# Differential attention on one core: the order of the work in each attention unit is replaced by two fixed orders

## The chip, the cores and the metric

The kernel runs on one core of a Trainium2 chip. The metric is the device time of one execution in microseconds (us), lower is better. The core has a matrix engine (TensorE, PE in the profile), three engines for elementwise work (VectorE = DVE, ScalarE = ACT, GpSimd = POOL), and a queue for transfers (SyncE = SP). Each engine runs its own instructions in program order and waits on semaphores for the others. [...]

## The reference, cut to what matters

The program is a two-layer trunk (attention, MLP, S5, MLP). The change touches only layer 0's attention, which is differential attention: each head has two score maps, and the second softmax, times a factor, is subtracted from the first.

```python
s = jnp.einsum('bqhcd,bkhcd->bhcqk', q, k).astype(jnp.float32)   # c = 0, 1
p = jax.nn.softmax(s, axis=-1)
w = p[:, :, 0] - lam * p[:, :, 1]
o = jnp.einsum('bhqk,bkhe->bqhe', w.astype(v.dtype), v)
return rmsnorm(o, subln_g) * (1.0 - lambda_init)
```

There are 8 heads, 1024 latent tokens and 256 context tokens (1280 keys), and 128 value columns per head. Context queries see the context keys alone. The queries and keys of a head are projections of the normed input by 128 columns of `attn_w_qkv`, and those of latent tokens are rotated (rope).

## The kernel before

Every fp32 product is done as three fp32r matmuls of split operands (high and low half; `mm3`, lines 131 to 134), so each operand is split by `split` (line 137: a copy on ACT gives the high half; line 138: a subtraction on DVE or POOL gives the low half).

`phase_b` runs the attention. It goes through 72 units, `n = 9h + u`: per head `h` one unit `u = 0` for the 256 context queries and eight units `u = 1..8` of 128 latent queries each. Two units (1 and 2, 3 and 4, and so on) form a pair of 256 queries; `pair = (u+1)//2`. In a unit these things happen, and in this program's "manual" section the order in which they are written is the order on PE, DVE, ACT and POOL; transfers are issued on SP:

- **scores** (line 579): both score maps. Map 0 fills PSUM columns 0 to 1279 (banks 0, 1 and half of 2), map 1 columns 1792 to 3071 (half of bank 3, banks 4 and 5). 18 matmuls for u > 0, 12 small ones for u = 0.
- **maxima** (line 592, or 588 for u = 0): DVE copies each map to SBUF and takes its row minimum (queries are negated).
- **exps** (line 602, or 599): ACT takes the exponential of each map with its row sum.
- **combine** (lines 610, 611, 613): DVE forms `w = p0 - lam * p1` for all 1280 keys.
- **parts**: the weights `w` of the unit *before* are transposed by PE (`w_part`, lines 620 and 625) in three pieces: key tiles 0-3 (w0), 4-5 (w1), 6-9 (w2). w0 is split straight from PSUM by `w_direct` (631 ACT, 632 DVE); w1 and w2 are copied to SBUF by ACT (`w_copy`, 638) and split by POOL (641, 642).
- **values** (lines 132 to 134, 256 columns): for a finished pair, weights times V into columns 0 to 255 of bank 6 (`pb`); `pair_out` copies the result out (732, ACT), POOL squares it (733), and `pair_sums` sums the squares by two one-column matmuls into bank 6 (739) and a copy (740, ACT). Pairs 1, 2, 3 are due in units 4, 6, 8, pair 0 in unit 2, and pair 4 in unit 1 of the next head.
- **projections**: in units 0, 1, 2, 3, 5, 7 the next head's keys and queries are projected (`proj_group`, `AHEAD`), eight products of three matmuls into bank 7, in up to three slices called fills (`FILLS`). Groups of context tokens (units 1 and 2) are split `direct`ly (523 ACT, 524 DVE). The others go through `evac` (528 ACT and 529 DVE empty the bank, and four transfers swap halves), `sine` (534 POOL), `add` (537 DVE) and `store` (137 ACT, 138 DVE). These later steps are queued in `post` and taken by `next_post`.
- **norm_pair** (772 DVE, 137 ACT, 138 POOL, two transfers): the norm of the previous head's pairs, in units 7 and 8 and 0 to 2 of the next head, from head 1's unit 7 on.

Units 4, 6 and 8 have values and no projection (`inside`): w0 goes to bank 7 there, between the two halves of the values. In the other units w0 goes to columns 1280 to 1791 (`whole`: halves of banks 2 and 3), which the scores leave free but whose banks they share. In head 7 there is nothing left to project; from `n = 64` on the output projection of heads 0 to 5 (`wo_group`, bank 7, emptied by 851) takes the place of the projections.

Of the kernel before, what the change touches and what calls it, by code (L numbers as in the profile page):

```python
# [6 lines left out]
F32 = mybir.dt.float32  # L7
# [63 lines left out]
class Prog:  # L71
# [431 lines left out]
    def proj_group(self, h, T, g, wt):  # L503

        nc = self.nc
        n, c0 = self.G_TOK[g], (256, 768, 0)[g]
        b = self.qb.next()[:, 0:n]
        scale = 1.0 if T else -0.125
        t = slice(c0 - 256, c0 + 256)
        hT = self.hT[g]  # L510
        q, sw, qc = self.rq, self.rs, self.rc
        hi, lo = (self.stg[:, j, 0:n] for j in range(2)) if h == 0 else self.operand(h, T, g)

        def product(k):
            return lambda: self.mm3(b, wt[k][0], wt[k][1], hT[0][:, k], hT[1][:, k], k == 0, k == 7)

        def out():
            if h == 0:
                for j, x in enumerate((hi, lo)):
                    self.dma((self.Kd if T else self.Qd)[j, :, c0 : c0 + n], x.bitcast(F32))  # L520

        def direct():
            nc.scalar.activation(hi, b, AF.Copy, scale=scale)
            nc.vector.scalar_tensor_tensor(lo, b, scale, hi.bitcast(F32), ALU.mult, ALU.subtract)  # L524
            out()

        def evac():
            nc.scalar.activation(q, b, AF.Copy, scale=scale)
            nc.vector.scalar_tensor_tensor(qc, b, scale, self.cosT[:, t], ALU.mult, ALU.mult)
            for j in range(4):  # L530
                self.dma(sw[32 * j : 32 * j + 32], q[32 * (j ^ 1) : 32 * (j ^ 1) + 32])

        def sine():
            nc.gpsimd.tensor_tensor(sw, sw, self.sinT[:, t], ALU.mult)

        def add():
            nc.vector.tensor_tensor(qc, qc, sw, ALU.add)

        def store():
            self.split(hi, lo, qc)  # L540
            out()

        return [product(k) for k in range(8)], [direct] if g == 2 else [evac, sine, None, add, store]


    def lam_setup(self):
# [103 lines left out]

    WO_BANKS = {8: 0, 9: 1, 0: 2, 1: 3, 2: 4, 3: 5, 4: 7}
    AHEAD = {0: (1, 0), 1: (1, 2), 2: (0, 2), 3: (1, 1), 5: (0, 0), 7: (0, 1)}
    FILLS = {0: (0, 3, 8, 8), 1: (0, 0, 8, 8), 2: (0, 4, 8, 8)}

    def b_start(self):

        self.rq, self.rs, self.rc = self.fv(0, 512), self.fv(2, 512), self.fv(4, 512)
        self.cosT, self.sinT = self.wv(8, 1024), self.wv(12, 1024)
        self.raw = Ring([self.wv(0, 1024), self.wv(4, 1024)])
        self.wr = Ring([(self.rv(4 * i, 4, 128), self.rv(4 * i + 2, 4, 128)) for i in range(3)])  # L660
        self.stg = self.rv(12, 2, 512)
        self.qb = Ring([self.bank(i) for i in (4, 5)])
        splits = [self.proj_weights(0, 1), self.proj_weights(0, 0)]
        self.dma(self.cosT, self.I["cos_t"])
        self.dma(self.sinT, self.I["sin_t"])
        post = []
        for split, T in zip(splits, (1, 0)):
            split(0)
            wt = split(1)
            for g in (2, 0, 1):  # L670
                products, rest = self.proj_group(0, T, g, wt)
                for f in products:
                    f()
                for f in post:
                    f()
                rest[0]()
                post = [f for f in rest[1:] if f]
                yield
        for f in post:
            f()  # L680

    def phase_b(self):
# [38 lines left out]
        def values(h, pair, k0=0, k1=10):  # L721
            V = loaded[h, "v"]
            last = 2 if pair == 0 else 10
            for kt in range(k0, min(k1, last)):
                self.mm3(pb[:, 0:256], V[0][:, kt], V[1][:, kt], self.wT[0][:, kt], self.wT[1][:, kt],
                         kt == 0, kt == last - 1)
# [9 lines left out]

        def pair_sums(h, pair):
            for i in range(2):
                mm(pb[:, 256 + i : 257 + i], sq[:, 128 * i : 128 * i + 128], self.ones, start=True, stop=True)
            nc.scalar.activation(hst[:, 1, h, 2 * pair : 2 * pair + 2], pb[:, 256:258], AF.Copy)  # L740


        def norm_calc(h, q0=0, q1=10):
# [25 lines left out]
        def norm_pair(h, pair):  # L769
            i = nloaded.pop(0)  # L770
            (nob, nrb), (nhi, nlo) = nbufs[i], nsplit[i]
            nc.vector.scalar_tensor_tensor(nob, nob, self.sg, nrb, ALU.mult, ALU.mult)
            self.split(nhi, nlo, nob, nc.gpsimd)
            for j, t in enumerate((nhi, nlo)):
                self.dma(self.on[h, j, :, 256 * pair : 256 * pair + 256], t.bitcast(F32))

        cols7 = ((2, 0), (0, 0), (0, 256), (1, 0), (1, 256))
        buf6 = [(nob, nrb), (self.wv(6, 256), self.wv(7, 256))]
# [88 lines left out]
        def next_post():  # L867
            f = post.pop(0) if post else None
            if f:
                f()  # L870

        with self.manual():
            for n in range(72 + 5):
# [10 lines left out]
                if front:  # L884
# [6 lines left out]
                        groups = [self.proj_group(h + 1, *a, wts[a[0]]) for a in (self.AHEAD[u],)] if u in self.AHEAD else []  # L891
                    self.scores(u, queries(pair), Ks[h % 2])
                    self.maxima(u, p, sm)
                if front:
                    if u == 8 and h < 6 or n == 0:
                        qsplit = self.proj_weights(h + 2 if n else 1, 0)
                    if u == 5 and h < 6:
                        ksplit = self.proj_weights(h + 2, 1)
                if 64 <= n < 74:
                    groups = [wo_group(wo_order[n - 64])]  # L900
                fills = [[], [], []]
                if h >= 7 and groups:
                    a = (0, 2, 4, 6) if late else (0, 4, 6, 6)
                    fills = [groups[0][0][a[i] : a[i + 1]] for i in range(3)]
                elif groups:
                    a = self.FILLS.get(u, (0, 4, 8, 8))
                    fills = [groups[0][0][a[i] : a[i + 1]] for i in range(3)]

                def fill(i):
                    for f in fills[i]:  # L910
                        f()

                def part(i):
                    if i < parts:
                        tb = pb[:, 256:512] if i == 1 else self.bank(7) if i == 0 and not groups else self.PS[:, 1280:1792]
                        return self.w_part(prev[1], prev[2], i, tb)

                def copied(w):
                    return self.w_copy(*w) if w else lambda: None

                inside = late and not groups and parts == 3
                if pv:
                    values(*pv, 0, 5 if inside else 10)
                fill(0)
                if front:
                    self.exps(u, 0, p, sm, s0, sn)
                while sums and sums[0][0] <= n:
                    sums.pop(0)[1]()
                w0 = part(0)
                next_post()  # L930
                if parts == 3:
                    self.w_direct(*w0)
                if inside:
                    values(*pv, 5)
                w1 = part(1)
                w2 = part(2) if inside else None
                if front:
                    self.exps(u, 1, p, sm, s0, sn)
                if inside:
                    halves2 = copied(w2)  # L940
                if pv:
                    pair_out(*pv)
                    sums.append((n + 1, lambda a=pv: pair_sums(*a)))
                    if pv[0] == 7:
                        tail.append((n + 1, pv[1]))
                if inside:
                    halves2()
                if front:
                    self.combine(u, p, s0, sn)
                if parts == 1:  # L950
                    self.w_direct(*w0)
                copied(w1)()
                fill(1)
                if not inside:
                    copied(part(2))()
                fill(2)
                if front and n - 7 >= 9 and (n - 7) % 9 < 5 and (n - 7) // 9 < 7:
                    norm_pair((n - 7) // 9 - 1, (n - 7) % 9)
                rest = groups[0][1] if groups else [None]
                if len(rest) == 1 and rest[0]:  # L960
                    rest[0]()
                todo7, run7 = run7, []
                for f in todo7:
                    f.pop(0)()
                    if f:
                        run7.append(f)
                if front and u == 0:
                    next_post()
                next_post()
                if len(rest) > 1:  # L970
                    rest[0]()
                    post += rest[1:]
                if h < 7 and u < 2:
                    wts[0] = qsplit(u)
                if h < 6 and u in (6, 7):
# [491 lines left out]
    def halves(self, src, slot):  # L1467
        self.split(slot[:, 0], slot[:, 1], src)
        return slot
# [1129 lines left out]
```

## Time and profile before

| what | value |
|---|---|
| time, median of 3 runs | 2877.79 us (2875.0 to 2881.31) |
| the profiled execution's own time | 2875.86 us |
| its span in the profile | 2874.1 us |
| PE busy | 2726.4 us (95%) |
| DVE, ACT, POOL busy | 2027.9 (71%), 1367.3 (48%), 1051.3 (37%) |
| the attention units (first score matmul to the end of unit 71) | from 216.7 to about 882 us |

Rows of the profile give the line of the kernel, the engine, the operation, and output and inputs by tile names (PS is PSUM, F, FC, W and R are SBUF areas), then partitions x elements. "x" is a count. A busy PE is not PE at its peak, since matmuls are pipelined and their ends are modelled. A row "A <- B" of the waits says that A sat idle until B was done.

### The profile page before, as it was taken

Reading aid. Unit: us, or ns where it says so; the run is one execution under the profiler, and the core shown is the slowest. Engines: PE = TensorE matmul, PEld = TensorE weight load, DVE = VectorE, ACT = ScalarE, POOL = GpSimd, SP = SyncE. Lnnn points to the kernel's source line nnn. Section 1 sums busy time; section 2 is a strip of 40 time slices with the busy share of each in tenths; the row PEclk is TensorE's granted clock in tenths of the full one; section 3 lists DMA queues with packets and bytes.
Section 4 is the critical chain, followed back from the end, with each engine's and each line's share of the span. In section 5 each row is a group of like instructions: output and inputs, shape, how many; then the busy total and the mean of one; then the engine's idle time right before and its main releaser. Section 6 shows DMA issues by size and latency. Waiting matters only on the chain. (4 is left out here: it accounts for less than half of the span.)

```text
span 2874.1 us, 43751 instructions
## 1 busy us (share of the span) xinstructions
PE 2726.4 (95%) x15645; PEld 2258.7 (79%) x15645; DVE 2027.9 (71%) x2984; ACT 1367.3 (48%) x2584; POOL 1051.3 (37%) x902
## 2 busy tenths in 40 slices
PE   6999988899888999999999999899999999999999
PEld 4787877777777787878877778788887778878887
DVE  6357777777775477766698878799633597668566
ACT  3425555555553763333344445477443633344443
POOL 3315665666654710000030004588221243336414
PEclk9999999999999999999999999899999999999999
DMA  9953123222524448887699878479843144467544
GB/s 281 323 176 115 60 87 90 91 80 64 179 85 138 150 147 303 296 300 255 211 326 318 277 238 274 154 230 274 285 140 109 60 157 162 161 228 240 163 133 143
DMA packets 377448, 539.13 MB, mean 188 GB/s; under 512 B 38286, under 2 KB 231052, under 8 KB 374028
## 3 DMA queue, kind: packets, MB, share of 16 engines
q1 hardware_dynamic: 377228, 536.32, 57.5%
q8 instruction: 123, 2.02, 0.3%
q14 instruction: 97, 0.79, 0.1%
HBM read 367.54 MB, written 164.47 MB: 185 GB/s over the span
## 5 line engine op out<-in xcount | busy, mean ns | idle before, releaser
L132 PE MATMUL PS<-H 128*128 128x512 f32 x1072 | 420.7, 393 | 3.1 <-ACT H L137 2.3
L134 PE MATMUL PS<-H 128*128 128x512 f32 x1072 | 417.7, 390 | 3.4 <-DVE H L138 2.1
L133 PE MATMUL PS<-H 128*128 128x512 f32 x1072 | 417.9, 390 | 0.0
L132 PE MATMUL PS<-H,R 128*128 128x512 f32 (+1 forms) x828 | 307.9, 374 | 15.6 <-DVE R L524 11.7
L133 PE MATMUL PS<-H,R 128*128 128x512 f32 (+1 forms) x828 | 300.8, 363 | 0.0
L134 PE MATMUL PS<-H,R 128*128 128x512 f32 (+1 forms) x828 | 299.8, 363 | 0.0
L602 ACT ACTIVATE F<-F,stat 128x1280 f32<-128x1280 f32 x128 | 174.2, 1361 | 168.3 <-DVE F L592 168.2
L132 PEld LDWEIGHTS PS<-H 128*128 128x128 f32 x1072 | 201.2, 188 | 50.7 <-issue 6.2
L134 PEld LDWEIGHTS PS<-H 128*128 128x128 f32 x1072 | 201.2, 188 | 46.7 <-DVE H L138 2.9
L133 PEld LDWEIGHTS PS<-H 128*128 128x128 f32 x1072 | 201.3, 188 | 40.6
L132 PE MATMUL PS<-R,H 128*128 128x512 f32 x534 | 212.2, 398 | 6.0 <-ACT H L137 3.3
L137 ACT ACTIVATE H<-U 128x640 fp32r<-128x640 f32 x216 | 132.1, 675 | 174.0 <-PE PS L133 146.6
L137 ACT ACTIVATE R<-W 128x512 fp32r<-128x512 f32 (+1 forms) x185 | 129.6, 708 | 174.7 <-PE PS L133 107.9
L134 PE MATMUL PS<-R,H 128*128 128x512 f32 x534 | 210.6, 396 | 1.8 <-DVE H L138 1.8
L133 PE MATMUL PS<-R,H 128*128 128x512 f32 x534 | 209.5, 393 | 0.0
L138 DVE TENSOR_TENSOR H<-U,H 128x640 fp32r<-128x640 f32 x216 | 165.2, 799 | 53.0 <-ACT H L137 51.2
L138 DVE TENSOR_TENSOR H<-W,H 128x512 fp32r<-128x512 f32 (+1 forms) x137 | 129.3, 954 | 99.0 <-ACT H L137 98.5
L132 PEld LDWEIGHTS PS<-H,R 128*128 128x128 f32 x828 | 158.8, 192 | 48.1 <-DVE R L524 13.4
L592 DVE TENSOR_SCALAR_CACHE_REDUCE F<-PS 128x1280 f32<-128x1280 f32 x128 | 185.1, 1483 | 5.5 <-PE PS L579 5.5
L137 ACT ACTIVATE H<-W 128x512 fp32r<-128x512 f32 (+2 forms) x158 | 95.5, 613 | 189.7 <-PE PS L133 116.9
L134 PEld LDWEIGHTS PS<-H,R 128*128 128x128 f32 x828 | 158.6, 192 | 25.3 <-issue 0.8
L133 PEld LDWEIGHTS PS<-H,R 128*128 128x128 f32 x828 | 158.7, 192 | 21.1
(528 smaller groups left out, 6776.2 us busy)
## 6 DMA issues: line engine op xcount, KB each, us to landing
W<-in_mlp_w SPq DMA_DIRECT2D x176, 256.0 KB, 3.5
U<-Aa SPq DMA_DIRECT2D x108, 320.0 KB, 4.5
Aa<-FU SPq DMA_DIRECT2D x91, 320.0 KB, 4.7
Ad<-F SPq DMA_DIRECT2D x112, 256.0 KB, 2.9
W<-Ad SPq DMA_DIRECT2D x112, 256.0 KB, 2.7
FU<-in_mlp_w SPq DMA_DIRECT2D x32, 512.0 KB, 6.0
Ta<-FU SPq DMA_DIRECT2D x16, 1024.0 KB
U<-in_ada_w SPq DMA_DIRECT2D x32, 512.0 KB, 12.3
```

The source lines that it names most:

```text
L132: mm(out, ah, bh, start=first, stop=False, **kw)
L133: mm(out, ah, bl, start=False, stop=False, **kw)
L134: mm(out, al, bh, start=False, stop=last, **kw)
L137: self.nc.scalar.activation(hi, src, AF.Copy)
L138: (lo_eng or self.nc.vector).tensor_tensor(lo, src, hi.bitcast(F32), ALU.subtract)
L592: ts(p[c], self.PS[:, 1792 * c : 1792 * c + 1280], 1.0, None, ALU.mult, ALU.min, accum_out=sm[:, c : c + 1])
L602: nc.scalar.activation(p[c], p[c], AF.Exp, bias=sm[:, c : c + 1], scale=-1.0, accum_out=sn[:, 0:1] if c else s0[:, u + 1 : u + 2])
```

## The change

The body of the loop over the units is written out in two fixed orders, chosen per unit.

Units with `late` values (u = 1, 4, 6, 8; 73 after the heads), or with the weights of a unit 0 to transpose: scores and maxima; values, w0 (bank 7 between the halves of the values in units 4, 6, 8; else `whole`), w1, w2 on PE; exp 0, a step of `post`, exp 1, `pair_out`, another step of `post`, the norm's multiplication, combine, and only then the split of w0 (`direct`) and the copies of w2 and w1, and the fills. Before, in units 4, 6 and 8, w0 was split ahead of combine.

All others (u = 0, 2, 3, 5, 7; 72): scores and maxima; values of pair 0 in u = 2; the first fill; w0, now into bank 6 (`low`); its split ahead of the exps (between them in u = 2 comes exp 0); a step of `post`; exps; the second fill; w2 to `whole` and then w1 (bank 6, or bank 7 in u = 2), the copies of both, and then the `pair_sums` that are due; combine; the third fill; the norm's multiplication.

In both, the projection's last step comes behind (`evac` or `direct`), then the norm's split and stores, which were ahead of it. `post` steps are no longer taken at the unit's end: `sine` and `add` fall in the same unit (1, 4, 6, 8), and `store` in the one after. The sums of pair 4 are taken in the same unit 1. The fills change: before (0,3,8,8) in u = 0, (0,0,8,8) in 1, (0,4,8,8) in the others; now (0,1,5,8) in 0, (0,0,0,8) in 1, (0,2,8,8) in 2, (0,0,5,8) in the others; a tuple holds the slice bounds of the three fills.

No instruction of arithmetic is added or removed.

```diff
--- before.py
+++ after.py
@@ -540,7 +540,7 @@
             self.split(hi, lo, qc)
             out()
 
-        return [product(k) for k in range(8)], [direct] if g == 2 else [evac, sine, None, add, store]
+        return [product(k) for k in range(8)], [direct] if g == 2 else [evac, sine, add, store]
 
 
     def lam_setup(self):
@@ -650,7 +650,7 @@
 
     WO_BANKS = {8: 0, 9: 1, 0: 2, 1: 3, 2: 4, 3: 5, 4: 7}
     AHEAD = {0: (1, 0), 1: (1, 2), 2: (0, 2), 3: (1, 1), 5: (0, 0), 7: (0, 1)}
-    FILLS = {0: (0, 3, 8, 8), 1: (0, 0, 8, 8), 2: (0, 4, 8, 8)}
+    FILLS = {0: (0, 1, 5, 8), 1: (0, 0, 0, 8), 2: (0, 2, 8, 8)}
 
     def b_start(self):
 
@@ -674,7 +674,7 @@
                 for f in post:
                     f()
                 rest[0]()
-                post = [f for f in rest[1:] if f]
+                post = rest[1:]
                 yield
         for f in post:
             f()
@@ -736,8 +736,8 @@
 
         def pair_sums(h, pair):
             for i in range(2):
-                mm(pb[:, 256 + i : 257 + i], sq[:, 128 * i : 128 * i + 128], self.ones, start=True, stop=True)
-            nc.scalar.activation(hst[:, 1, h, 2 * pair : 2 * pair + 2], pb[:, 256:258], AF.Copy)
+                mm(pb[:, i : i + 1], sq[:, 128 * i : 128 * i + 128], self.ones, start=True, stop=True)
+            nc.scalar.activation(hst[:, 1, h, 2 * pair : 2 * pair + 2], pb[:, 0:2], AF.Copy)
 
 
         def norm_calc(h, q0=0, q1=10):
@@ -770,9 +770,13 @@
             i = nloaded.pop(0)
             (nob, nrb), (nhi, nlo) = nbufs[i], nsplit[i]
             nc.vector.scalar_tensor_tensor(nob, nob, self.sg, nrb, ALU.mult, ALU.mult)
-            self.split(nhi, nlo, nob, nc.gpsimd)
-            for j, t in enumerate((nhi, nlo)):
-                self.dma(self.on[h, j, :, 256 * pair : 256 * pair + 256], t.bitcast(F32))
+
+            def halves():
+                self.split(nhi, nlo, nob, nc.gpsimd)
+                for j, t in enumerate((nhi, nlo)):
+                    self.dma(self.on[h, j, :, 256 * pair : 256 * pair + 256], t.bitcast(F32))
+
+            return halves
 
         cols7 = ((2, 0), (0, 0), (0, 256), (1, 0), (1, 256))
         buf6 = [(nob, nrb), (self.wv(6, 256), self.wv(7, 256))]
@@ -891,7 +895,6 @@
                         groups = [self.proj_group(h + 1, *a, wts[a[0]]) for a in (self.AHEAD[u],)] if u in self.AHEAD else []
                     self.scores(u, queries(pair), Ks[h % 2])
                     self.maxima(u, p, sm)
-                if front:
                     if u == 8 and h < 6 or n == 0:
                         qsplit = self.proj_weights(h + 2 if n else 1, 0)
                     if u == 5 and h < 6:
@@ -899,77 +902,112 @@
                 if 64 <= n < 74:
                     groups = [wo_group(wo_order[n - 64])]
                 fills = [[], [], []]
-                if h >= 7 and groups:
-                    a = (0, 2, 4, 6) if late else (0, 4, 6, 6)
+                if groups:
+                    a = self.FILLS.get(u, (0, 0, 5, 8))
+                    if n > 71:
+                        a = (0, 2, 4, 6) if n == 72 else (0, 4, 6, 6)
                     fills = [groups[0][0][a[i] : a[i + 1]] for i in range(3)]
-                elif groups:
-                    a = self.FILLS.get(u, (0, 4, 8, 8))
-                    fills = [groups[0][0][a[i] : a[i + 1]] for i in range(3)]
+                inside = late and not groups
+                low, high, last, whole = pb[:, 0:512], pb[:, 256:512], self.bank(7), self.PS[:, 1280:1792]
 
                 def fill(i):
                     for f in fills[i]:
                         f()
 
...
+                def part(i, tb):
+                    return self.w_part(prev[1], prev[2], i, tb) if i < parts else None
+
+                def direct(w):
+                    if w:
+                        self.w_direct(*w)
+
+                def copied(*ws):
+                    for f in [self.w_copy(*w) for w in ws if w]:
+                        f()
+
+                def exps(c):
+                    if front:
+                        self.exps(u, c, p, sm, s0, sn)
+
+                def output(*a):
+                    pair_out(*a)
+                    sums.append((n + (parts != 1), lambda: pair_sums(*a)))
+                    if a[0] == 7:
+                        tail.append((n + 1, a[1]))
+
+                def do_sums():
+                    while sums and sums[0][0] <= n:
+                        sums.pop(0)[1]()
+
+                def norm():
+                    if front and n - 7 >= 9 and (n - 7) % 9 < 5 and (n - 7) // 9 < 7:
+                        return norm_pair((n - 7) // 9 - 1, (n - 7) % 9)
+
+                if late or parts == 1:
+                    if n == 73:
+                        fill(0)
+                    if inside:
+                        values(*pv, 0, 5)
+                        w0 = part(0, last)
+                        values(*pv, 5)
+                        w1, w2 = part(1, high), part(2, whole)
+                    else:
+                        if pv:
+                            values(*pv)
+                        w0, w1 = part(0, whole), part(1, high)
+                    exps(0)
+                    next_post()
+                    exps(1)
+                    if pv:
+                        output(*pv)
+                    next_post()
+                    split = norm()
+                    if front:
+                        self.combine(u, p, s0, sn)
+                    direct(w0)
+                    if inside:
+                        copied(w2, w1)
+                    else:
+                        copied(w1)
+                        if n != 73:
+                            fill(0)
+                        fill(1)
+                        copied(part(2, whole))
+                        fill(2)
+                        do_sums()
+                else:
+                    if pv:
+                        values(*pv)
+                        output(*pv)
+                    fill(0)
+                    w0 = part(0, low)
+                    if pv:
+                        exps(0)
+                    direct(w0)
+                    next_post()
+                    if not pv:
+                        exps(0)
+                    exps(1)
+                    fill(1)
+                    w2 = part(2, whole)
+                    w1 = part(1, last[:, 256:512] if pv and h < 7 else self.bank(0)[:, 0:256] if n == 72 else high)
+                    copied(w2, w1)
+                    do_sums()
+                    if front:
+                        self.combine(u, p, s0, sn)
+                    fill(2)
+                    split = norm()
+                if groups:
+                    rest = groups[0][1]
                     rest[0]()
+                    post += rest[1:]
+                if split:
+                    split()
                 todo7, run7 = run7, []
                 for f in todo7:
                     f.pop(0)()
                     if f:
                         run7.append(f)
-                if front and u == 0:
-                    next_post()
-                next_post()
-                if len(rest) > 1:
-                    rest[0]()
-                    post += rest[1:]
                 if h < 7 and u < 2:
                     wts[0] = qsplit(u)
                 if h < 6 and u in (6, 7):
```

More of the change, by code (lines that the diff above doesn't have):

```diff
@@ L911, in fill @@
                         f()
[L913 to L929, printed above, removed]
-                next_post()
[L931 to L960, printed above, removed]
+                def part(i, tb):
[3 more added lines that the diff above has]
+                        self.w_direct(*w)
@@ L966, in phase_b @@
                         run7.append(f)
-                if front and u == 0:
-                    next_post()
-                next_post()
-                if len(rest) > 1:
-                    rest[0]()
-                    post += rest[1:]
                 if h < 7 and u < 2:
```

## The prediction

> **What bounds the kernel now.** I read the stretch of the attention units first, split by head and, for head 4, by unit. (Columns: stretch, its length, then busy time and count of PE, its weight loads, DVE, ACT, POOL; granted clock; DMA share; GB/s.)
>
> ```profile
> 216.66:290.15 73.49, 68.86 (x483) 59.08 (x483) 54.43 (x88) 41.43 (x79) 38.89 (x35) 0.98 0.32 110
> 290.15:366.89 76.74, 74.34 (x533) 62.97 (x533) 60.68 (x97) 44.32 (x91) 49.89 (x47) 1.00 0.21 62
> 535.95:618.85 82.90, 75.22 (x532) 63.13 (x532) 65.74 (x101) 46.34 (x96) 54.23 (x52) 1.00 0.27 82
> 787.62:882.50 94.88, 83.30 (x535) 67.51 (x535) 68.82 (x108) 50.73 (x102) 55.11 (x59) 0.96 0.27 84
> ...
> 535.95:546.27 10.32, 8.65 (x51) 6.66 (x51) 9.28 (x22) 5.86 (x18) 8.18 (x9) 1.00 0.35 107
> 546.27:556.57 10.30, 9.33 (x77) 8.50 (x76) 7.08 (x10) 6.10 (x11) 6.22 (x6) 1.00 0.55 169
> 556.57:564.72 8.15, 7.65 (x65) 6.69 (x64) 6.10 (x10) 4.69 (x10) 2.02 (x2) 1.00 0.56 186
> 564.72:577.30 12.58, 9.57 (x58) 7.59 (x57) 9.78 (x14) 5.93 (x13) 6.96 (x8) 1.00 0.14 43
> 577.30:584.12 6.82, 6.82 (x59) 6.30 (x58) 5.72 (x9) 2.94 (x6) 4.50 (x4) 1.00 0.15 38
> 584.12:594.32 10.20, 9.73 (x58) 7.49 (x58) 8.09 (x13) 6.18 (x13) 7.77 (x7) 1.00 0.05 14
> 594.32:601.12 6.80, 6.80 (x59) 6.24 (x58) 5.49 (x8) 4.06 (x8) 4.81 (x5) 1.00 0.17 41
> 601.12:610.78 9.66, 9.51 (x58) 7.43 (x58) 7.66 (x13) 6.23 (x13) 7.66 (x9) 1.00 0.16 43
> 610.78:618.85 8.07, 7.17 (x59) 6.23 (x59) 6.53 (x8) 4.34 (x8) 6.11 (x6) 1.00 0.32 96
> ```
>
> The first four rows are heads 0, 1, 4 and 7, the nine below units 0 to 8 of head 4. PE sets the pace: units 4 and 6 have it busy throughout (6.82, 6.80). Everywhere else it waits, 7.7 us of head 4's 82.90. Next I asked whom it waits for in heads 1 to 6:
>
> ```profile
> PE PS L132 <- DVE R L524: 11.0, 7, 2.0
> PE PS L625 <- DVE F L592: 8.8, 18, 1.0
> PE PS L625 <- DVE FC L529: 5.5, 6, 0.9
> PE PS L620 <- DVE F L592: 4.9, 5, 1.0
> PE PS L625 <- ACT FC L740: 4.7, 6, 0.9
> PE PS L579 <- ACT F L638: 1.9, 6, 0.3
> ```
>
> In order: unit 3's projection waits for bank 7, which DVE's L524 empties late; transposes into `whole` wait for the maxima (units 2, 3, 5, 7, and L620 in unit 1); in unit 8 they wait for bank 7's emptying (L529); unit 0 waits for the copy of the sums (L740). The last row matters for the change: scores (L579) wait for the copy of `whole` (L638), whose columns they never write. So PE waits for a reader of the *bank*, not of the columns.
>
> **The durations used**, all of that stretch (groups with mean ns, then single events with start and length in us):
>
> ```profile
> L599 ACT ACTIVATE F<-F,stat 128x256 f32<-128x256 f32 x24 | 12.1, 505 | 1.9 <-DVE F L588 1.4
> L632 DVE TENSOR_TENSOR R<-PS,R 128x512 fp32r<-128x512 f32 x55 | 37.9, 689 | 28.5 <-ACT R L631 28.5
> L638 ACT ACTIVATE F<-PS 128x512 f32<-128x512 f32 x49 | 29.1, 593 | 43.3 <-POOL R L641 14.9 <-issue 12.8 <-POOL FC L144 7.4
> L638 ACT ACTIVATE F<-PS 128x256 f32<-128x256 f32 x49 | 18.6, 380 | 0.0
> L537 DVE TENSOR_TENSOR FC<-FC 128x512 f32<-128x512 f32 x24 | 19.5, 811 | 0.0
> L772 DVE SCALAR_TENSOR_TENSOR F<-F,lamc 128x256 f32<-128x256 f32 x13 | 9.0, 689 | 0.0
> ```
> ```profile
> 564.72 2.02 PE L579 MATMUL PS<-R 64*128 64x512 f32 x18
> 583.38 0.82 PE L625 MATMUL PS<-ident,F 128*128 128x128 f32 x6
> 587.43 0.40 PE L132 MATMUL PS<-H,R 128*128 128x512 f32 x1
> 588.12 0.40 PE L132 MATMUL PS<-H,R 128*128 128x512 f32 x1
> 589.51 0.50 PE L739 MATMUL PS<-lamc,adat 128*128 128x1 f32 x4
> ```
> ```profile
> 577.95 0.59 ACT L528 ACTIVATE FC<-PS 128x512 f32<-128x512 f32 x1
> 582.60 1.30 POOL L534 TENSOR_TENSOR FC<-FC,W 128x512 f32<-128x512 f32 x1 [2.01 <-DMA FC<-FC]
> 588.91 1.49 DVE L592 TENSOR_SCALAR_CACHE_REDUCE F<-PS 128x1280 f32<-128x1280 f32 x1
> 590.32 0.09 DVE L592 DVE_READ_ACCUMULATOR F<-PS 128x1 f32 x1
> 591.43 1.36 ACT L602 ACTIVATE F<-F,stat 128x1280 f32<-128x1280 f32 x1
> 592.91 0.16 DVE L610 RECIPROCAL stat<-stat 128x1 f32<-128x1 f32 x1 [0.65 <-ACT F L602]
> 593.36 1.55 DVE L613 SCALAR_TENSOR_TENSOR F<-F,stat 128x1280 f32<-128x1280 f32 x1
> ```
>
> One maximum takes 1.41 us to the next (588.91 to 590.32), its exponential starts 0.1 behind it, and combine begins 1.48 behind the second exponential's start (591.43 to 592.91) and ends 2.0 later. A product of three matmuls takes 0.69 (587.43 to 588.12), a transpose 0.12 (six from 583.38 to unit 5's start at 584.12), the sums' small matmuls 0.4, and a value matmul 0.12, since unit 4 has 30 of them and ten transposes behind its scores: (6.82-2.0-1.2)/30. `sine` starts 4.06 us behind the end of the bank's emptying on ACT (577.95+0.59 to 582.60), held by the four swap transfers.
>
> **The change, part by part.** Zero of each timeline is its unit's first score matmul; "lo" is L632.
>
> *Units 4 and 6 (values).* Scores end at 2.0; the maxima, with only the bank's emptying (to about 1.5) ahead, run 2.1 to 4.9, and the second exponential starts at 5.0. The emptying on ACT ends at 0.8, so `sine` runs 4.9 to 6.2 and `add`, now in front of combine, to 7.0, half a microsecond past 6.5, where combine could have begun. Combine ends at 9.0, lo, now behind it, at 9.7. PE needs 6.8 as before and waits for nothing. So the next unit begins with its weights 2.2 late and bank 7 free only at 2.9. Change of these units: 0, with the next unit's scores over the late lo, and all of the delay on that unit if they were shorter, as in unit 0 below. The norm's split and its two stores, moved behind the bank's emptying and its four swaps on ACT, POOL and SP, can only let the swaps go earlier; their own data is read in head 7.
>
> *Units 5 and 7.* w0 starts at 2.25 instead of 2.0, the fill of five products waits to 2.9 and ends at 6.4. DVE takes the maxima behind lo, 2.9 to 5.7; the second exponential runs 5.8 to 7.15. Then ACT copies w2 (0.5) and w1 (0.4), to 8.1. PE has transposed both by 7.2. But next in its order stand the `pair_sums`, into bank 6, where w1 lies: by the bank row above they wait to 8.1, a new wait of 0.9, with the last three products queued behind. Sums 0.4 and products 2.1 end at 10.6, and unit 5's norm rows at 10.8: +0.6 for unit 5 (10.20), +0.95 for unit 7 (9.66). `store`, now a unit later, falls on DVE behind lo, in the 1.5 us of waiting for the second exponential; if it overran, combine (to 9.2) would still have 1.4 us under the last products. The old order had twelve matmuls in front of sums and transposes to cover all this. Even with the maxima at 2.1 the unit can't end before 9.9, so the pair costs between +0.2 and, with `add` later by 0.5, +2.5.
>
> *Unit 8.* The wait for L529 goes, since `store` no longer stands ahead of the maxima: 8.07 becomes 6.8, -1.27. But the norm's multiplication (0.69) is now in front of combine: combine ends at 9.6, lo at 10.3.
>
> *Unit 0.* Its first product needs bank 7, which holds unit 8's w0 until that lo: 10.3-6.8 = 3.5. Scores end at 0.9, so PE idles 2.5 us where it had 1.7 of shorter waits. From there: product 4.2, w0 4.7, four products 7.5, w2 and w1 8.2; ACT splits w0 and stores by 5.9, runs four small exponentials (0.5 each) to 7.9, waits for w2 and copies to 9.1; sums 9.5, three products 11.6: +1.3 against 10.32. Were lo 0.7 earlier (no norm), +0.6; with `add` 0.5 later, +1.8.
>
> *Unit 1.* The transposes come after 30 value matmuls, at 5.7, past the maxima (4.9): the wait of 1.0 goes, and the sums of pair 4 (0.4) come in: 9.6, -0.7. *Unit 2* loses those sums and both waits: scores 2.0, values 0.75, two products, w0, six products, w2, w1, in all 6.95: -1.2, and no engine that I can see holds it. *Unit 3* keeps a third of its wait: unit 2's norm and L524 end at 3.5 on DVE, so the fill starts then instead of at 4.05, and the sums wait to 8.7: 11.2, -1.4 (bounds -2.0 without the norm, -0.9 with L524 later).
>
> Sum for head 4: +1.3-0.7-1.2-1.4+0+0.6+0+0.95-1.27 = -1.7. Five heads (2 to 6) like it: -8.6 before rounding.
>
> *The clock.* Heads 2, 3 and 5 have a unit 0 at a lowered clock:
>
> ```profile
> 366.89:378.65 11.76, 10.09 (x51) 7.80 (x50) 9.43 (x22) 5.85 (x18) 8.51 (x9) 0.85 0.37 114
> 451.50:463.40 11.90, 10.19 (x52) 7.80 (x51) 9.42 (x22) 5.86 (x18) 8.51 (x9) 0.86 0.37 110
> 618.85:630.75 11.90, 10.21 (x51) 7.78 (x51) 9.41 (x22) 5.85 (x18) 8.15 (x9) 0.86 0.34 104
> ```
>
> Against head 4's 10.32 at full clock it costs up to 1.6 each time. Unit 3's single wait of 2.0 never lowered the clock in these heads; unit 0's two short waits around one-column matmuls and transposes did. In the new unit 0 the idle piece is one of 2.5 with full matmuls behind it. I take half of the three as gone, -2.4, between -4.8 (none left) and +3.2 (all five). [...]
>
> *Heads 0, 1, 7.* Heads 0 and 1 had little to win (PE busy 68.86 of 73.49, 74.34 of 76.74) and get the new waits. By the timelines without norms, head 1 comes to 80.0, +3.2; in head 0 units 3, 5 and 7 gain about 2.5 and unit 2 loses 0.5: +2. Head 7 (94.88, PE busy 83.30) has `wo` products for projections, whose bank ACT empties early; the same steps give about -3 (-8 to +3: its unit 8 now transposes ahead of the fills, and so waits for late maxima).
>
> Total: -8.6-2.4+3.2+2-3 = -8.8 us. The profiled execution took 2875.86, 1.8 more than its span of 2874.1; 2875.86-8.8 = 2867.1. The median of the runs shown is 1.9 higher; I split that and say **2868**.
>
> **The rivals.**
>
> *`add` comes late.* It was a unit later before, where nothing waited for it; now combine, lo, the next w0, bank 7 and the next maxima stand behind it. Against: in head 4 its swap took 4.06. For: in the rows before, transfers of other kinds share the queue, and POOL's squares and DVE's combine now fall together. Each microsecond more delays the units behind 4, 6, 8 and 1 by about 3.5 us a head, 24 in seven heads. From 0.4 more (4.5 us swaps) the gain is gone; at 0.7 the time is 2868+17 = 2885. This is the case that ends slower.
>
> *The sums don't wait*, because PE is later than ACT there or the maxima start at 2.1 in all projection units: about 0.9 in four units of seven heads, -25: 2843. Against it stands the 2.8 us of DVE work left over from the unit before.
>
> *The clock falls in every unit 0* and in the new waits besides: +3.2 for the five heads instead of -2.4, and about as much again in heads 1 and 7: 2868+9 = 2877, no change.
>
> **How the numbers follow.** Two times of this kernel that differ by less than 0.2% (5.8 us) can't be told apart here. Chances: my sum 0.5 (2858 to 2876), late `add` 0.22, no wait at the sums 0.12, the clock 0.16. The bounds of the terms added up reach 2845 and 2888; that range leaves out the tails of the second and the third case. Faster: four fifths of my sum, 0.4, the third case, 0.12, and a little of the clock's, 0.03: 0.55. Slower: 0.22 and 0.02 of the clock's: 0.24. No change: 0.21.
>
> **What would show it.** Right: L739 waiting for L638 in units 0, 3, 5 and 7, at 0.9; unit 0's L132 waiting about 2.5 for L632; units 8 and 2 at 6.8 and 7.0; no wait of PE for L529 or of L620 for the maxima. Wrong: `add` (L537) waiting more than a microsecond for L534; units 5 and 7 under 10.0; unit 3 under 10.5 or over 12; values in units 4, 6, 8 waiting for POOL's halves (L641, L642), which I hold to be ready a microsecond ahead.

## The result and the profile after

| | median of five runs | range |
|---|---|---|
| before | 2877.79 us | 2875.0 to 2881.31 |
| after | 2897.31 us | 2891.09 to 2902.69 |

The ratio is 1.0064, with a 95% interval of 1.0047 to 1.0082: the change costs 0.64%, where I had forecast a gain of about 10 us, and the time lies above my range. The profiled execution of after took 2897.7 us, 2.0 more than its span.

First the stretch of the units up to the start of unit 71 (columns as in the prediction), and unit 2 of head 0. Of before:

```profile
216.66:869.17 652.51, 596.28 (x4128) 499.71 (x4127) 502.48 (x783) 362.38 (x733) 408.69 (x387) 0.98 0.30 94
232.97:240.47 7.50, 7.05 (x59) 6.26 (x58) 4.63 (x7) 4.32 (x8) 2.53 (x2) 1.00 0.26 74
```

Of after, heads 0, 3 and 4 and the same stretch, and then units: seven of head 4 (units 4 and 6, 6.82 and 6.80, are left out), unit 2 of head 0, and units 0 of heads 2 and 3:

```profile
219.89:304.15 84.26, 72.11 (x484) 60.73 (x483) 54.49 (x89) 43.13 (x81) 36.93 (x35) 0.94 0.30 102
...
471.89:557.68 85.79, 76.11 (x532) 64.36 (x531) 61.85 (x103) 47.76 (x97) 51.90 (x51) 0.98 0.27 80
557.68:638.77 81.09, 74.19 (x533) 63.19 (x532) 61.79 (x103) 47.61 (x97) 51.33 (x51) 1.00 0.28 84
...
219.89:884.80 664.91, 594.52 (x4128) 503.44 (x4127) 479.29 (x783) 372.52 (x733) 391.91 (x387) 0.98 0.30 92
```
```profile
557.68:569.13 11.45, 8.50 (x52) 6.70 (x52) 9.45 (x23) 5.74 (x18) 8.46 (x10) 1.00 0.30 93
569.13:578.52 9.39, 9.39 (x82) 8.97 (x81) 6.67 (x10) 5.09 (x9) 4.34 (x5) 1.00 0.63 168
578.52:585.35 6.83, 6.83 (x59) 6.25 (x59) 5.40 (x9) 4.92 (x10) 2.60 (x3) 1.00 0.76 251
585.35:596.90 11.55, 9.75 (x57) 7.47 (x56) 8.37 (x14) 6.32 (x14) 7.97 (x7) 1.00 0.12 37
...
603.72:614.50 10.78, 9.69 (x59) 7.60 (x59) 8.61 (x13) 6.34 (x14) 9.44 (x8) 1.00 0.04 14
...
621.30:631.94 10.64, 9.58 (x57) 7.47 (x57) 9.59 (x13) 6.85 (x14) 8.59 (x8) 1.00 0.08 24
631.94:638.77 6.83, 6.83 (x60) 6.26 (x59) 4.45 (x7) 4.62 (x9) 4.65 (x6) 1.00 0.47 136
236.46:251.24 14.78, 9.25 (x60) 8.25 (x60) 8.98 (x14) 5.20 (x10) 3.10 (x3) 0.77 0.18 57
...
385.44:401.72 16.28, 10.22 (x52) 8.00 (x51) 9.90 (x23) 5.85 (x18) 9.49 (x11) 0.79 0.30 87
471.89:486.98 15.09, 10.10 (x51) 7.88 (x51) 9.75 (x23) 5.85 (x18) 8.71 (x10) 0.89 0.31 87
```

Head 4 is what I had drawn: 81.09 against 82.90. The loss sits in a few units that differ from it: unit 2 of head 0 takes 14.78 instead of 7.50, and units 0 of heads 2 and 3 take 16.28 and 15.09 where head 4's takes 11.45; smaller ones are unit 5 (13.28) and unit 0 (12.97) of head 6. In all the units up to the start of unit 71 are 12.4 us longer, and PE isn't busier (594.52 against 596.28): it waits.

The rest of the span is longer too, by 3.2 ahead of the units (219.89 against 216.66) and 6.0 from the start of unit 71 on (2010.9 against 2004.9, the spans less 884.80 and 869.17). Of the 6.0, 1.7 lies in unit 71, which was edited (13.33 before and 15.06 after, from its first matmul's start to its last one's); behind it only the units right after the heads were. In the profiles of the experiments below the two stretches differ by as much between kernels with nearly the same code there (216.4 to 222.3 us ahead of the units, 2003.0 to 2011.2 from unit 71 on), so I don't put the rest down to the change, and can't exclude that some of it follows from it.

For whom PE waits within the units of after:

```profile
PE PS L739 <- ACT F L638: 25.5, 31, 1.6
PE PS L132 <- DVE R L632: 17.7, 6, 5.3
PE PS L625 <- DVE F L613: 13.0, 21, 2.8
PE PS L579 <- DVE R L632: 6.3, 2, 5.5
```

The first row is the bank wait that I had forecast, 0.8 each (PSUM is one tile of 128 x 4096 fp32 columns in this kernel, taken as eight banks of 512). The other three are combine (L613) and the lo of w0 (L632) behind it, with single waits up to 5.5 us. What holds combine shows in the waits around one line, `sine` (L534), within the units: first of before, then of after.

```profile
POOL FC L534 <- DMA FC<-FC: 53.0, 23, 8.3
```
```profile
POOL FC L534 <- DMA FC<-FC: 80.6, 28, 9.0
...
DVE FC L537 <- POOL FC L534: 43.3, 28, 7.5
```

POOL already waited for the swap transfers before the change. But `add` (L537) never waited for `sine` in the units; now it does 28 times, 43.3 us in all, with combine queued behind it on DVE. The next two fences set a quiet passage beside a late one (ACT, POOL, DVE and PE from after's timeline, start and length in us). Quiet, into unit 0 of head 4:

```profile
550.96 0.60 ACT L528 ACTIVATE FC<-PS 128x512 f32<-128x512 f32 x1 [2.00 <-PE PS L134]
...
555.66 1.30 POOL L534 TENSOR_TENSOR FC<-FC,W 128x512 f32<-128x512 f32 x1 [1.36 <-DMA FC<-FC]
...
558.80 1.83 POOL L641 TENSOR_SCALAR R<-F 128x512 fp32r<-128x512 f32 x1 [0.25 <-ACT F L638]
...
556.99 0.69 DVE L537 TENSOR_TENSOR FC<-FC 128x512 f32<-128x512 f32 x1 [1.18 <-POOL FC L534]
...
558.60 1.55 DVE L613 SCALAR_TENSOR_TENSOR F<-F,stat 128x1280 f32<-128x1280 f32 x1
560.07 0.68 DVE L632 TENSOR_TENSOR R<-PS,R 128x512 fp32r<-128x512 f32 x1
...
560.81 0.50 PE L132 MATMUL PS<-H,R 128*128 128x512 f32 x1 [2.15 <-DVE R L632]
```

Late, into unit 0 of head 3:

```profile
465.19 0.60 ACT L528 ACTIVATE FC<-PS 128x512 f32<-128x512 f32 x1 [2.02 <-PE PS L134]
...
470.46 1.29 POOL L534 TENSOR_TENSOR FC<-FC,W 128x512 f32<-128x512 f32 x1 [1.96 <-DMA FC<-FC]
...
473.79 1.26 POOL L642 TENSOR_TENSOR R<-F,R 128x512 fp32r<-128x512 f32 x1
475.01 1.65 POOL L641 TENSOR_SCALAR R<-F 128x256 fp32r<-128x256 f32 x1
...
471.78 0.69 DVE L537 TENSOR_TENSOR FC<-FC 128x512 f32<-128x512 f32 x1 [1.75 <-POOL FC L534]
...
473.74 2.65 DVE L613 SCALAR_TENSOR_TENSOR F<-F,stat 128x1280 f32<-128x1280 f32 x1
476.32 0.68 DVE L632 TENSOR_TENSOR R<-PS,R 128x512 fp32r<-128x512 f32 x1
...
477.05 0.64 PE L132 MATMUL PS<-H,R 128*128 128x512 f32 x1 [4.19 <-DVE R L632]
```

Counted from the end of the bank's emptying (551.56 and 465.79), `sine` starts at 4.10 and 4.67, `add` at 5.43 and 5.99, combine at 7.04 and 7.95, lo at 8.51 and 10.53. The swaps are 0.57 late, lo 2.02. Most of the growth is combine itself, 2.65 instead of 1.55: it now starts together with POOL's halves. PE waits 4.19 instead of 2.15, the granted clock falls (0.89 in that unit, first matmul 0.64 instead of 0.50), and the unit is 3.6 longer than the quiet one.

### The profile page after: what moved, and what is told of

Its sections match the earlier page's. It is cut to its first block, busy times and chain, and to the rows that moved or that the text cites. A ratio compares the mean times of both kernels' runs of the same rounds, so it can differ in the third digit from the quotient of the medians.

```text
span 2895.7 us, 43780 instructions
## 1 busy us (share of the span) xinstructions
PE 2725.5 (94%) x15645; PEld 2261.2 (78%) x15645; DVE 1996.3 (69%) x2984; ACT 1377.0 (48%) x2584; POOL 1030.7 (36%) x902
## 3 DMA queue, kind: packets, MB, share of 16 engines
q8 instruction: 123, 2.02, 0.3%
## 5 line engine op out<-in xcount | busy, mean ns | idle before, releaser
L132 PE MATMUL PS<-H 128*128 128x512 f32 x1072 | 420.5, 393 | 3.0 <-ACT H L137 1.9
L132 PE MATMUL PS<-H,R 128*128 128x512 f32 (+1 forms) x828 | 308.1, 374 | 24.2 <-DVE R L632 17.7
L132 PEld LDWEIGHTS PS<-H 128*128 128x128 f32 x1072 | 201.2, 188 | 50.7 <-issue 6.2
L132 PE MATMUL PS<-R,H 128*128 128x512 f32 x534 | 213.1, 400 | 4.0 <-ACT H L137 3.3
L132 PEld LDWEIGHTS PS<-H,R 128*128 128x128 f32 x828 | 159.0, 192 | 55.2 <-DVE R L632 18.9
```

Source lines behind the costliest of these rows:

```text
L132: mm(out, ah, bh, start=first, stop=False, **kw)
```

## The experiments

The theory: `add`, put directly ahead of combine, passes on the lateness of the swaps. Beside it I kept two other causes of loss: the split of w0 behind combine in units 4, 6 and 8 (unit 0's wait for L632), and the `pair_sums` waiting for a copy in their bank. Each was undone alone, then all three. The first four are edits of the changed kernel, measured beside before (2876.63) on one chip.

**`add` behind combine.** The second step of `post` in the units with late values goes behind combine and the split.

```diff
-                    next_post()
                     split = norm()
                     if front:
                         self.combine(u, p, s0, sn)
                     direct(w0)
+                    next_post()
```

> The changed kernel with one edit: in the units with values, DVE's add (L537) is taken behind combine and the split of the unit's weights instead of ahead of combine. Theory S (late swaps): the changed order costs time only where the four swap transfers land late (unit 2 of head 0 took 14.8 us, unit 0 of heads 2 and 3 16.3 and 15.1, unit 5 of head 6 13.3, against 6.8, 11.4 and 10.8 in other heads), since add holds combine there. Then these excesses, about 20 us with the slow clock behind them, go, and the half microsecond by which add delays combine elsewhere: about 2872 us (2865 to 2880). Rival B (bank waits): the loss is that of the new waits that stand in every head, for the copy ahead of the pair sums (25 us) and for the late split of w0 (18 us); then this edit brings little: 2888 to 2897.

2877.98 us, ratio to before 1.0008 (0.9996 to 1.0020): 19.3 below after, so the loss against the kernel before is gone by this one line. The gain of 10 us that I had forecast isn't there either. Heads 3 and 4 of it:

```profile
463.14:544.87 81.73, 74.48 (x533) 63.15 (x533) 63.19 (x102) 47.45 (x97) 52.82 (x51) 1.00 0.28 85
544.87:626.58 81.71, 74.46 (x532) 63.16 (x532) 63.58 (x102) 47.41 (x97) 52.84 (x51) 1.00 0.27 83
```

Head 3 now equals head 4: in heads 2 to 6 the disturbed units are gone, but for some 1.2 us in head 2 (82.91). Unit 2 of head 0 still takes 10.59, against 7.50 before the change. It isn't `add`'s own length that was saved, since head 4 itself got 0.6 worse: `add` now stands ahead of the next maxima, and units 5 and 7 take 11.25 and 11.14.

**w0 split between the exps again, in units 4, 6, 8.**

```diff
                     exps(0)
+                    if inside:
+                        direct(w0)
                     next_post()
...
-                    direct(w0)
+                    if not inside:
+                        direct(w0)
```

> The changed kernel with one edit: in units 4, 6 and 8 the split of w0 (L631, L632) stands between the two exponentials again, as it did before the change, so bank 7 is free ahead of combine. Theory S: in quiet heads unit 0 loses its wait of 2.0 us for L632 down to the wait for combine that follows it (about 1.3 less, 6 heads), while late swaps go on holding combine: 2885 to 2892. Rival B: the waits for L632 (18 us in six units) were the loss: 2877 to 2882.

2888.78 us, 1.0038 (1.0024 to 1.0052): 8.5 below after. PE no longer waits at L132 for L632 (17.7 us in after), but its wait for combine doubles:

```profile
PE PS L625 <- DVE F L613: 26.2, 27, 3.8
PE PS L579 <- DVE R L632: 5.1, 2, 5.0
```

The lateness stays and only meets PE at another instruction. The split's place is a cost of its own, and not what makes the units late.

**`pair_sums` behind the last products**, in the units with projections.

```diff
                     copied(w2, w1)
-                    do_sums()
                     if front:
                         self.combine(u, p, s0, sn)
                     fill(2)
+                    do_sums()
```

> The changed kernel with one edit: in the projection units the pair sums (L739) come behind the third fill instead of ahead of it, so PE runs the last products while ACT copies w1. Both theories: the wait of L739 for L638 (0.8 us in about 30 units, 25 us) goes; the sums' copy then falls into the next unit's scores. If it is paid at once in PE time: 2873 (2868 to 2880). If DVE or ACT is the real pace and the wait only moves on: 2888 to 2897. The excesses of theory S stay, in the same heads.

2878.67 us, 1.0002 (0.9988 to 1.0016): 18.6 below after. The bank wait was worth what it showed:

```profile
PE PS L625 <- DVE F L613: 18.6, 21, 4.0
PE PS L132 <- DVE R L632: 18.0, 6, 4.9
...
PE PS L739 <- ACT F L638: 1.8, 1, 1.8
```

25.5 us of it became 1.8, while combine's row grew from 13.0 to 18.6, which takes 5.6 of the 23.7 back. The waits for L632 are as long as in after. This edit alone makes up the loss against the kernel before as well; but its wait was a term of my sum, and the late `add` was not.

**All three.**

> The three edits together. Theory S: what each brings adds up, less the part of the split's that add's move has already brought: 2897 - 25 - 24 - 4 = about 2845 (2838 to 2860), faster than the kernel before. Rival B without theory S: 2860 to 2872.

2851.06 us, 0.9902 (0.9882 to 0.9921): 46.3 below after, faster than both kernels. The single effects sum to 19.3+8.5+18.6 = 46.4. Head 4, and the units up to the start of unit 71:

```profile
526.39:602.80 76.41, 73.07 (x533) 63.48 (x533) 64.16 (x102) 46.92 (x97) 53.65 (x51) 1.00 0.29 89
...
216.68:836.97 620.29, 581.02 (x4128) 501.23 (x4128) 500.12 (x783) 366.80 (x733) 404.18 (x386) 0.99 0.32 99
```

The next three kernels make the suspected cause larger. Two transfers of 32 rows of the projection to unused memory go on SP ahead of the four swaps of each group of heads 1 to 7; they change nothing that is computed. This edit was put on the changed kernel, on the kernel before, and on the kernel with all three edits, beside before at 2876.26.

```diff
+            for _ in range(2 if h else 0):
+                self.dma(self.extra[self.nextra], q[0:32])
+                self.nextra += 1
             for j in range(4):
                 self.dma(sw[32 * j : 32 * j + 32], q[32 * (j ^ 1) : 32 * (j ^ 1) + 32])
```

**Swaps later, on the changed kernel.** (Line numbers here are 3 higher: L616 is combine, L635 lo, L742 the sums, L641 the copy.)

> The changed kernel with two more small transfers (64 KB each, from the emptied bank's copy to a buffer that nothing reads) issued ahead of each group's four swaps, in heads 1 to 7's projections; at about 0.6 us each on SP they make the swaps, sine and add some 1.2 us later. Theory S: behind units 4, 6 and 8 that delay stands on the path in each head, some 3 x 7 x 1.2 = 25 us, and up to a microsecond more for each place where combine falls together with POOL's work: 2920 to 2945. If late swaps are not what costs (rival B): within 5 us of 2897.

2946.51 us, 1.0241 (1.0224 to 1.0258): 49 more than after, a little over what I expected, for about 0.9 us of lateness (the median from emptying to `sine` goes from 4.05 to 4.93).

```profile
PE PS L628 <- DVE F L616: 37.0, 21, 3.9
PE PS L132 <- DVE R L635: 28.1, 6, 5.4
PE PS L742 <- ACT F L641: 23.4, 28, 1.8
```

Combine and lo cost 65 us of waiting instead of 31, while the bank wait of the sums stays. PE is also busy 16.6 us longer with the same matmuls (611.15 against 594.52 up to the start of unit 71), at a granted clock of 0.95 instead of 0.98. So about 56 us are lost per us of lateness, where the prediction's rival had 24.

**Swaps later, on the kernel before.**

> The kernel before with the same two transfers ahead of the swaps. There add is taken a unit later (10.6 to 14 us behind the emptying), so by theory S the delay lies in slack: 2874 to 2884. If the transfers themselves cost time (SP, the transfer engines), this run shows it: it would be slower by as much as the run above.

2891.59 us, 1.0049 (1.0034 to 1.0064): 15 more. I had expected nearly nothing, and that was wrong: the old order is less sensitive (16 us per us), not insensitive. The units up to the start of unit 71:

```profile
216.38:881.92 665.54, 604.22 (x4128) 506.10 (x4128) 508.41 (x783) 362.27 (x733) 408.98 (x387) 0.97 0.32 98
```

The units are 13.0 longer than before's; in 7.9 of them PE is busy, with the same matmuls at a lower granted clock (0.97), and in 5.1 it waits. What lowers the clock there, the later `sine` on POOL or the transfers themselves, wasn't separated.

**Swaps later, with all three edits.**

> The kernel with the three edits, with the same two transfers ahead of the swaps. add stands behind combine and the split there, about 3 us behind the end of sine: by theory S no change, 2847 to 2858. If add's place were not what protects it: 2870 or more.

2858.69 us, 0.9936 (0.9921 to 0.9951): 7.6 above the kernel with all three edits, and 0.7 above the range that I expected. With `add` behind combine the same two transfers, which here make `sine` 0.7 later, cost about a sixth of what they do in the changed order. If the 8 to 15 us of these two kernels are taken off the 49, an estimated 34 to 42 go with its place.

**Other fills**, on the kernel with all three edits, to cover its remaining wait of transposes for combine (22.7 us).

```diff
-    FILLS = {0: (0, 1, 5, 8), 1: (0, 0, 0, 8), 2: (0, 2, 8, 8)}
+    FILLS = {0: (0, 2, 5, 8), 1: (0, 0, 0, 8), 2: (0, 2, 8, 8), 5: (0, 2, 5, 8), 7: (0, 2, 5, 8)}
```

> The kernel with the three edits, with two products ahead of the first transposes in units 0, 5 and 7 (one in unit 0 before, none in the others). In the trace of the three edits PE waits 22.7 us for combine (L613) ahead of those transposes, about 0.6, 1.0 and 0.5 us in units 0, 5 and 7; bank 7 is free there since its split stands ahead of combine. If the wait is filled: 7 to 14 us less, about 2840 (2836 to 2846). If DVE paces these units, so that the wait moves behind the fill: 2848 to 2853.

2848.79 us, 0.9901 (0.988 to 0.9921), no difference from 2851.06. The wait moved:

```profile
PE PS L625 <- DVE F L592: 5.3, 9, 1.7
PE PS L625 <- DVE R L632: 5.2, 15, 2.7
PE PS L625 <- DVE F L613: 5.1, 7, 2.2
```

Combine's 22.7 us became 5.1, but the waits for the maxima and for lo went from 5.7 together to 10.5, and two more, for the copies of the values and of w1, from 2.0 to 8.2: 11.0 of the 17.6 came back. So the time isn't set by the number of products in front. That DVE alone paces these units, as I had expected for this outcome, isn't shown: 6.2 of the 11.0 is waiting for ACT's copies.

## Why the prediction was wrong

**What held.** The timelines. Head 4's nine units were to change by -1.7 and changed by -1.81; unit 0 was to take 11.6 (11.45), unit 1 9.6 (9.39), unit 2 6.95 (6.83), unit 3 11.2 (11.55), units 5 and 7 10.8 and 10.6 (10.78, 10.64), unit 8 6.8 (6.83). The sums wait for the copy in their bank, 25.5 us in 31 waits, and moving them gained 18.6. Unit 0 waits for lo, 2.15 in head 4. No wait for L529 is left, and the values wait for no halves of POOL. Of my signs of being wrong one came: `add` waits for `sine` by more than a microsecond. But it does so in quiet head 4 too (1.18), and my timeline of units 4 and 6 had such a wait in it (maxima to 4.9, `sine` to 6.2), so I had set that sign too low.

**The step that failed** is "`sine` starts 4.06 us behind the end of the bank's emptying", one event of head 4 that I took for every group. From it `add` had half a microsecond of its own cost and no more. In after, 21 of the 28 groups in the units keep to it (3.9 to 4.2), and seven start 4.7 to 10.8 behind. Where the swaps came later, combine and lo came later still, and PE stood up to 5.5 us. The spread was there to see in the profile before: over its 28 groups `sine` starts 3.9 to 10.2 behind the emptying, the middle one at 4.6 (five of them held by something else than the transfers), and one row of the old timeline shows a wait of 8.33:

```profile
234.13 1.28 POOL L534 TENSOR_TENSOR FC<-FC,W 128x512 f32<-128x512 f32 x1 [8.33 <-DMA FC<-FC]
```

That group lies in head 0, and the matching one in after, at 10.8, makes its unit 2 last 14.78. It cost nothing before because `add` came a unit later.

**By the terms of the sum**, for the units of the profiled executions: heads 2 to 6 were to give -11.0 with the clock and gave -1.2; head 0 +2 and gave +10.8, 7.3 of it in unit 2; head 1 +3.2 and +4.6; head 7 -3 and -1.7 to the start of unit 71, which unit 71 itself gives back. With `add` moved behind combine, heads 2 to 6 come to -10.9. So for these heads the sum fits an order without the late swaps, though in part by two errors that cancel: no fall of the clock is left there, and units 5 and 7 cost 0.5 more each. The other terms were too good even without them: head 0 then gives +6.6 instead of +2, head 1 +4.3 instead of +3.2, and head 7 -0.4 to the start of unit 71 instead of -3. Most of head 0's lies in units 2, 5 and 7 (10.59, 11.18 and 11.12, against 7.50, 9.11 and 10.30 before). Together that is 8.3 of the 10 us by which this kernel stands above my 2868; what was missed in each of these terms, no run separates.

**The clock term** was -2.4 and came to about nothing: the granted clock of the units is 0.98 in both traces. Unit 0 of head 5 lost its fall, but units 0 of heads 2 and 3 still have one, now beside long waits (0.79 and 0.89 in the rows above), and so has unit 2 of head 0 (0.77). Unit 0 of head 6 has a new one, 0.87, though its swaps were on time (`sine` at 4.04) and PE's longest wait in it is 2.08 (2.15 in head 4's, which kept its clock); it takes 12.97. With `add` behind combine, heads 2 to 6 have 1.00 throughout. What brings the clock down these runs don't show. In after it fell in the units with PE's longest waits, 5.5 (unit 2 of head 0), 5.26 and 4.19 (units 0 of heads 2 and 3), but also in head 6's. In before no wait in heads 1 to 6 is over 2.0, and units 0 of heads 2 to 6 all have the same two short ones (0.8 and 0.9): the clock fell in heads 2, 3 and 5 (0.85, 0.86, 0.86) and stayed at 1.00 in heads 4 and 6. So that these two waits lower it, as I had read those rows, isn't shown either.

**The rival** "`add` comes late" was the right mechanism, with its place and its direction, and I gave it 0.22 where the spread of the old groups spoke for more. Its price was low as well: 24 us per us, from passing a delay on one to one to the units behind, against 56 measured, or some 39 to 47 (an estimate) without the 8 to 15 us that the same transfers cost in the two other kernels; in the passage above 0.57 became 2.02 at lo and 3.6 in the unit. The rival on sums that don't wait did not come about, and of the rival on the clock in every unit 0 three of five units did (heads 2, 3 and 6).

## What to carry to other kernels

A step that waits for a transfer belongs behind the work that the bound engine needs next, however little it costs when the transfer is on time; ask of the whole group of such events, with its longest, not of one event in a quiet place. Here `add`'s place was worth 19.3 us. When several orders change at once, undo each alone: here two regressions of 19 us each, and one of 8, hid an order that is worth 26 us without them.

## What the runs showed of the hardware

DVE's 128x1280 combine, `scalar_tensor_tensor` with both inputs in SBUF, takes 1.55 us alone (577.24 in after, with POOL idle), and 2.65 where it starts at the same time as POOL's 1.26 us subtraction on SBUF operands; in the quiet passage it is POOL's conversion of 128x512 that stretches, to 1.83 us from the 0.70 that it takes just ahead of the late passage's combine, when combine starts 0.2 us ahead of it. In both passages one of the two seems to stand for most of the other's time: in the late one it is 1.34 from the end of POOL's subtraction (475.05) to combine's end (476.39), nearly combine's whole length alone; in the quiet one it is 0.48 from combine's end (560.15) to that of POOL's conversion (560.63), two thirds of its 0.70. Which was first the trace can't tell in the late one (473.74 and 473.79). That they hold each other up is my reading of these overlaps: no run moved this work of POOL by itself.

The swaps, four transfers of 64 KB within SBUF on one queue, let `sine` start 4.1 us behind the emptying in the quiet passage, 4.67 in the late one, and over 10 in head 0. In head 0 the four were issued only 2.0 to 5.0 us behind the emptying (0.1 to 1.9 in the quiet passage), behind loads on the same queue. Why the other single groups come late was not settled.
